# Fewer weights split ahead, their loads on another queue, and a new order of the attention and what follows

## The chip, the cores and the metric

The kernel runs on one core of one Trainium2 chip. The metric is the time of one execution on the device, in microseconds (us): before the change a median of 1505.86 us over three runs (1504.99 to 1508.77). Engines are named as in the profile: PE (TensorE, matmuls), PEld (its weight loads), DVE (VectorE), ACT (ScalarE), POOL (GpSimd) and SP (SyncE). SP and POOL start the transfers (DMAs); each takes its own in order and stands still when one has to wait.

## The reference

A model of two layers over 512 latent and 256 context tokens of width 1024 (one batch, fp32). Both layers normalise, scale and shift by a vector made from a condition, mix, project back and add to the residual:

```
for layer in range(2):
    sh, sc, ga = split(silu(c) @ w_mod[layer] + b_mod[layer])     # for latents, and for the context with c_ctx
    h = rms_norm(x, g_pre[layer]) * (1 + sc) + sh
    layer 0: xv, g_hy, q, k, v, g_att = split(h @ e_w_in)
             y = concat(hyena(xv) * silu(g_hy), attention(q, k, v) * silu(g_att)) @ e_w_out
    layer 1: q, k, v, o, z, gates = split(h @ o_w_in)
             y = (rms_norm(mlstm_forward + mlstm_backward) * silu(z)) @ o_w_out    # latents only
    x = x + ga * rms_norm(y, g_post[layer])
```

The attention has 8 query heads and 2 key and value heads of 128; `hyena` is a short convolution and a long one of the sequence's length; the mLSTM of layer 1 has 8 heads with keys of 128 and values of 256, computed in chunks, with `sigmoid(o)` on its output.

## The kernel before

Every fp32 product is made of three faster ones: both operands are split into a high part (fp32r) and the rest, and `mm3` (L1021) adds high by high, high by low and low by high. Activations are split as they come, weights once each: `split` (L1011) is a CAST on ACT and a subtraction on DVE. The usual way of a weight tile of 1024 x 256 is `load_w` (L1036): two loads of 512 KB by SP into one of three `wr` buffers, two casts of 128x1024 into `wh`, two subtractions into `wl`.

The work stands in regions: start, hyena (hy), attention (att), the output of layer 0 (out0), two parts of layer 1 (l1a, l1b) and its output (out1). Each region is first recorded and then issued by `play` (L999) in the order of a table, `ORDERS` (L157), a permutation of the recorded work over all engines at once; a second table, `SLOTS` (L736), says which buffer of a pool each tile takes. All rows of the profile thus have the line L1006, and an engine works in the order that the table gives it. A wait in front of one instruction holds all that stand behind it on that engine or queue.

In the attention, three more things run beside it: weights of the next region, the vectors of the condition (`w_mod`, 1 MB tiles loaded by SP in pairs named wh and wl, and used by PE as they are, in products into `pm`), and `split_ahead` (L1898). This takes weights of layer 1 (o_w_in, named `ow`) and splits them early, since layer 1 has less room on ACT and DVE. One block is two of the eight k-tiles of a head's tile: `G.dma_start` (POOL) loads 256 KB into one of three places in `yacc0`, which the attention does not need; at the next call ACT casts it and DVE subtracts, in place, and POOL writes both halves to `w_scratch` in memory, from which the place is free again. `ahead` (L1894) lists the blocks: (head h, tile t, k), from head 1 on, without the first four: 52 blocks. The loop of 24 attention steps calls it three times a step (L2094). In the rows a load is `yacc<-in_o_w_in`, the cast and the subtraction are `yacc<-yacc`, the write is `w_scratch<-yacc`.

Layer 1 reads these back by `load_split` (L2266), two transfers of 1 MB by SP, in `Head.load` (L2429, the tile with queries and keys) and `Head.load_v` (L2432, the values).

The attention's own chain is: products into `pj`, CAST to `PTh` on ACT, subtraction to `PTl` on DVE, products of both by PE. `qjunk` is a sum of squares that ACT makes for the norm of the queries, `qTh`/`qTl` are the split queries, `hdh`/`hdl` the probabilities, and `dec` is a result that SP writes to `y_scratch`. In the output stages `hf` is the scaled and shifted transposed input, `xn` the normalised one.

Of the kernel before, what the change touches and what calls it, by code (L numbers as in the profile page):

```python
# [14 lines left out]
P = 128  # L15
# [136 lines left out]
class Ctx:  # L152
# [669 lines left out]
        2,  # L822
    ],
    "mrow@5": [
        0, 1, 0, 1, 0, 1, 0, 1,
    ],
    "xt@9": [
        1, 0, 1, 0, 1, 0, 1,
# [81 lines left out]
def _body(tc, ins, outs):  # L910
# [1160 lines left out]
    for n in range(24):  # L2071
# [22 lines left out]
        for _ in range(3):  # L2094
            split_ahead()
# [734 lines left out]
```

## Time and profile before

| what | value |
|---|---|
| median of three runs | 1505.86 us |
| the profiled execution | 1511.4 us, span 1509.6 us |
| PE busy | 1459.5 us, 97% of the span |
| DVE, ACT, POOL busy | 1079.8, 788.6, 179.9 us |
| mean granted clock of the core | 0.992 |
| attention, 410 to 720 us of the span | PE 294.0, DVE 227.8, ACT 166.2, POOL 101.8 us busy |
| yacc casts and w_scratch writes | 52 and 104 |

Busy time is from the instructions of each engine. The span is the profiled execution from its first to its last instruction; the rest of its time lies around it. The granted clock is a share of the full 2.4 GHz, so 0.5 is 1.2 GHz. A matmul's end is modelled, so its duration overlaps the next one's start.

### The profile page before, as it was taken

To read this page: it belongs to the slowest core of one execution; us is meant where nothing else is said; L and a number is where in the kernel's file an instruction comes from. 1 tells how busy PE (TensorE), PEld (TensorE's weight loads), DVE (VectorE), ACT (ScalarE), POOL (GpSimd) and SP (SyncE) were. 2 spreads that over 40 slices of the span, in tenths; PEclk is the share of its full clock that TensorE was granted. 3 is DMA by queue.
4 is the path that set the end of the run, shared out by engine and by line. 5 is a ranking of instruction groups with operands and counts; after the bars stand their busy time and mean duration, and the time that the engine had idled before them with its cause. 6 is when DMAs were issued, how large, how long until landed. Compare 5 with 4: busy or idle time off the path is not lost.

```text
span 1509.6 us, 26392 instructions
## 1 busy us (share of the span) xinstructions
PE 1459.5 (97%) x10266; PEld 1335.3 (88%) x10266; DVE 1079.8 (72%) x1986; ACT 788.6 (52%) x1608; POOL 179.9 (12%) x297
## 2 busy tenths in 40 slices
PE   7999999999998998999999989999999999999997
PEld 5889999889997897888998779999999999988985
DVE  6688787887866777779424889776666878789445
ACT  6633344334445554556332557555446777778432
POOL 1101001101114343421000100000000101000000
PEclk9999999999999999999999999999999999999999
DMA  9788677779656677663463234887765657674561
GB/s 378 227 196 204 187 200 163 197 207 210 141 167 213 221 250 233 238 234 119 149 226 107 102 127 127 270 282 246 237 227 194 247 209 256 241 254 145 202 229 59
DMA packets 86990, 306.51 MB, mean 203 GB/s; under 512 B 10907, under 2 KB 19611, under 8 KB 80624
## 3 DMA queue, kind: packets, MB, share of 16 engines
q1 hardware_dynamic: 65816, 233.24, 44.5%
q0 software_dynamic: 20176, 70.40, 19.0%
q8 instruction: 81, 1.33, 0.3%
q10 hardware_dynamic: 872, 1.18, 0.2%
q14 instruction: 45, 0.37, 0.1%
HBM read 247.60 MB, written 103.32 MB: 232 GB/s over the span
## 4 chain that ended last, share of the span: by engine, by line
PE 73%; DVE 9%; DMA 7%; issue 4%; ACT 4%; POOL 2%; SPq 0%; POOLq 0%; DVEq 0%; ACTq 0%
PE pj L1006 54%; PE pm L1006 17%; DMA yacc<-in_o_w_in 3%; DMA w_scratch<-yacc 2%; DVE hh L1006 1%; PE s L1006 1%; DVE wl L1006 1%; POOL w_scratch L1006 1%; DMA oz_scratch<-so 1%; ACT wh L1006 1%; DVE yacc L1006 1%; DVE num L1006 1%; DVE cvo L1006 0%; ACT hf L1006 0%; DMA decay<-nc_scratch 0%
## 5 line engine op out<-in xcount | busy, mean ns | idle before, releaser
L1006 PE MATMUL pj<-hTh,wh 128*128 128x512 f32 (+1 forms) x832 | 287.1, 347 | 1.7 <-DVE qTl L1006 1.4
L1006 PE MATMUL pj<-wh,hTh 128*128 128x256 f32 (+2 forms) x1008 | 286.5, 291 | 1.8 <-ACT wh L1006 1.0
L1006 PE MATMUL pj<-wl,hTh 128*128 128x256 f32 (+2 forms) x1008 | 285.3, 290 | 2.0 <-DVE wl L1006 2.0
L1006 PE MATMUL pj<-hTl,wh 128*128 128x512 f32 (+1 forms) x832 | 285.8, 345 | 0.4 <-DVE hTl L1006 0.4
L1006 PE MATMUL pj<-hTh,wl 128*128 128x512 f32 (+1 forms) x832 | 285.7, 345 | 0.0
L1006 PE MATMUL pj<-wh,hTl 128*128 128x256 f32 (+2 forms) x1008 | 285.1, 290 | 0.0
L1006 DVE TENSOR_TENSOR wl<-wr,wh 128x1024 fp32r<-128x1024 f32 (+1 forms) x126 | 152.3, 1213 | 70.3 <-ACT wh L1006 70.2
L1006 PEld LDWEIGHTS pj<-wh,hTh 128*128 128x128 f32 x1008 | 189.3, 190 | 6.4 <-issue 1.6
L1006 PEld LDWEIGHTS pj<-wl,hTh 128*128 128x128 f32 x1008 | 189.8, 190 | 5.4 <-DVE wl L1006 2.6
L1006 PEld LDWEIGHTS pj<-wh,hTl 128*128 128x128 f32 x1008 | 189.4, 190 | 3.5 <-issue 1.7
L1006 ACT CAST wh<-wr 128x1024 fp32r<-128x1024 f32 (+1 forms) x126 | 130.0, 1042 | 91.5 <-PE pj L1006 53.1
L1006 PEld LDWEIGHTS pj<-hTh,wh 128*128 128x128 f32 x832 | 156.9, 189 | 19.8 <-issue 2.0
L1006 PEld LDWEIGHTS pj<-hTl,wh 128*128 128x128 f32 x832 | 157.3, 189 | 17.8 <-DVE hTl L1006 0.7
L1006 PEld LDWEIGHTS pj<-hTh,wl 128*128 128x128 f32 x832 | 156.9, 189 | 17.9
L1006 POOL DMA_DIRECT2D o_sums<-in_o_w_in x44 | 35.8, 819 | 322.6 <-DMA o_sums<-in_o_w_in 161.4
L1006 DVE TENSOR_TENSOR wl<-ch,wh 128x1024 fp32r<-128x1024 f32 x44 | 53.6, 1219 | 28.7 <-ACT wh L1006 28.7
L1006 POOL DMA_DIRECT2D w_scratch<-yacc x104 | 56.8, 549 | 88.3 <-DVE yacc L1006 43.3
L1006 POOL TENSOR_SCALAR_AFFINE_SELECT decay<-decay 128x512 f32<-128x512 f32 x16 | 13.2, 829 | 410.9 <-DMA decay<-nc_scratch 384.1
L1006 ACT CAST wh<-ch 128x1024 fp32r<-128x1024 f32 x44 | 46.0, 1046 | 29.5 <-PE pj L1006 9.8
L1006 ACT CAST PTh<-pj 128x384 fp32r<-128x384 f32 (+1 forms) x80 | 34.9, 459 | 37.8 <-PE pj L1006 37.4
L1006 DVE TENSOR_TENSOR PTl<-pj,PTh 128x384 fp32r<-128x384 f32 (+1 forms) x80 | 40.6, 524 | 14.2 <-ACT PTh L1006 13.8
L1006 DVE TENSOR_TENSOR yacc<-yacc 128x512 fp32r<-128x512 f32 x52 | 35.5, 686 | 18.0 <-ACT yacc L1006 18.0
(381 smaller groups left out, 3609.9 us busy)
## 6 DMA issues: line engine op xcount, KB each, us to landing
wr<-in_e_w_in SPq DMA_DIRECT2D x52, 512.0 KB, 5.7
w_scratch<-yacc POOLq DMA_DIRECT2D x104, 256.0 KB, 4.0
o_sums<-in_o_w_in POOLq DMA_DIRECT2D x44, 512.0 KB, 8.3
ch<-o_sums SPq DMA_DIRECT2D x33, 512.0 KB, 4.1
wr<-in_o_w_in SPq DMA_DIRECT2D x30, 512.0 KB, 5.2
yacc<-in_o_w_in POOLq DMA_DIRECT2D x52, 256.0 KB, 4.1
wh<-w_scratch SPq DMA_DIRECT2D x13, 1024.0 KB, 7.3
wl<-w_scratch SPq DMA_DIRECT2D x13, 1024.0 KB, 7.7
```

What stands on the lines that cost most here:

```text
L1006: x = fn(*a, **k)
```

## The change

- `ahead` holds heads 2 to 6 alone: 40 blocks where there were 52. The second tile of head 1 and both of head 7 are now loaded and split as other weights (`load_w`, with two more loads of 512 KB, casts and subtractions for each tile). `w_scratch` shrinks to five heads.
- The loads of the blocks are issued by SP; the writes stay with POOL. The program has 134 transfers on POOL where it had 210, and 480 on SP where it had 440.
- An attention step calls `split_ahead` twice instead of three times (before the order of the table).
- The tables of order of att, out0, l1a, l1b and out1, and many buffer numbers, are new. PE has the same matmuls.

```diff
     "att": [
-        75, 76, 77, 78, 79, 45, 46, 47, 48, 49, 50, 51, 52, 53, 54, 55, 56, 57, 58, 59, 60, 61, 62, 63, 64, 65, 66, 67, 68, 80, 81, 82, 83, 15, 16,
+        15, 16, 17, 18, 19, 20, 21, 22, 23, 24, 25, 26, 27, 28, 29, 30, 31, 32, 33, 34, 35, 36, 37, 38, 2, 0, 3, 45, 46, 47, 48, 49, 50, 51, 52, 53,
...
-    wsd = nc.dram_tensor("w_scratch", [8, 2, 2, P, KT, 256], F32).ap()
-    ahead = [(h, t, k) for h in range(1, 8) for t in range(2) for k in range(0, KT, 2)][4:]
+    wsd = nc.dram_tensor("w_scratch", [5, 2, 2, P, KT, 256], F32).ap()
+    ahead = [(h, t, k) for h in range(2, 7) for t in range(2) for k in range(0, KT, 2)]
...
-                G.dma_start(wsd[h, t, i][:, k:k + 2], f(x))
+                G.dma_start(wsd[h - 2, t, i][:, k:k + 2], f(x))
...
-            G.dma_start(f(lo), ow[4 * h + t][:, k:k + 2])
+            SP.dma_start(f(lo), ow[4 * h + t][:, k:k + 2])
...
-        for _ in range(3):
+        for _ in range(2):
...
-            SP.dma_start(f(x), wsd[h, t, i])
+            SP.dma_start(f(x), wsd[h - 2, t, i])
...
-            self.w = w_next if self.h == 1 else load_split(self.h, 0) if self.h else load_w(ow[0])
+            self.w = w_next if self.h == 1 else load_split(self.h, 0) if 1 < self.h < 7 else load_w(ow[4 * self.h])
...
-            self.wv = load_split(self.h, 1)
+            self.wv = load_split(self.h, 1) if 1 < self.h < 7 else load_w(ow[4 * self.h + 1])
```

Three places show how the instructions move. The first is SP's queue in the attention, around the first pair of `w_mod` tiles (wh_829 and wl_830; dec is written out ahead of them, wr are weights of later regions). Before:

```order
L1006 DMA wr_4606<-in_e_w_in 128x1024
L1006 DMA wr_4597<-in_e_w_in 128x1024
L1006 DMA y_scratch<-dec_4367 128x768
L1006 DMA wh_829_4553<-in_w_mod 128x2048
L1006 DMA wl_830_4554<-in_w_mod 128x2048
L1006 DMA wr_4652<-in_e_w_in 128x1024
```

And now, from this pair to the second one (wl_957 and wh_956):

```order
L1006 DMA y_scratch<-dec_4367 128x768
L1006 DMA wl_830_4554<-in_w_mod 128x2048
L1006 DMA wr_4606<-in_e_w_in 128x1024
L1006 DMA wh_829_4553<-in_w_mod 128x2048
L1006 DMA yacc_600_4321<-in_o_w_in 128x512 x2
L1006 DMA wr_4645<-in_e_w_in 128x1024
...
L1006 DMA yacc_600_4321<-in_o_w_in 128x512
L1006 DMA wr_4733<-in_e_w_in 128x1024
L1006 DMA wl_957_4681<-in_w_mod 128x2048
L1006 DMA yacc_600_4321<-in_o_w_in 128x512
L1006 DMA wh_956_4680<-in_w_mod 128x2048
L1006 DMA yacc_600_4321<-in_o_w_in 128x512 x4
```

The loads of the blocks stand among SP's transfers, two of them right behind the first pair, one between the two tiles of the second.

The second place is ACT in the attention, around the four casts into one PTh tile (PTh_4570; hdh and hdl are probabilities of one row of tokens). Before:

```order
L1006 CAST PTh_4570<-pj_4572 128x3x128
L1006 CAST PTh_4570<-pj_4573 128x3x128
L1006 CAST PTh_4570<-pj_4582 128x3x128
L1006 CAST yacc_600_4321<-yacc_600_4321 128x512
L1006 CAST PTh_4570<-pj_4581 128x3x128
L1006 CAST wh_871_4595<-wr_4597 128x1024
```

And now:

```order
L1006 CAST PTh_4570<-pj_4572 128x3x128
L1006 ACTIVATE hdh_4365,sm_4576<-s_850_4574,mx_4575,rq_4504 128x256
L1006 CAST yacc_600_4321<-yacc_600_4321 128x512
L1006 CAST PTh_4570<-pj_4573 128x3x128
L1006 ACTIVATE hdl_4366,sm_4585<-s_859_4583,mx_4584,rq_4504 128x256
L1006 CAST PTh_4570<-pj_4581 128x3x128
L1006 CAST PTh_4570<-pj_4582 128x3x128
```

A cast of a block still stands between the casts of one PTh tile, with three of these behind it where there was one.

The third place is DVE late in the heads of layer 1, at the end of a chunk (num is its numerator, dn its denominator, C and Cl the state of the mLSTM and its low part, vl the low part of values). Before:

```order
L1006 SCALAR_TENSOR_TENSOR dn_12958<-num_2231_12928 128x4
L1006 TENSOR_TENSOR dn_12958<-dn_12958,cq_1360_9530 128x4
L1006 RECIPROCAL dn_12958<-dn_12958 128x4
L1006 SCALAR_TENSOR_TENSOR C_12978<-C_12973,apb_9531,pj_12974 128x258
L1006 TENSOR_TENSOR Cl_12976<-C_12973,Ch_12975 128x258
L1006 TENSOR_TENSOR Cl_12981<-C_12978,Ch_12980 128x258
L1006 SCALAR_TENSOR_TENSOR C_12984<-C_12978,apb_9531,pj_12979 128x258
L1006 SCALAR_TENSOR_TENSOR C_12990<-C_12984,apb_9531,pj_12985 128x258
L1006 SCALAR_TENSOR_TENSOR num_2273_12970<-pm_12983,cq_1360_9530,num_2273_12970 128x258
```

And now:

```order
L1006 SCALAR_TENSOR_TENSOR dn_12900<-num_2233_12870 128x4
L1006 TENSOR_TENSOR dn_12900<-dn_12900,cq_1360_9470 128x4
L1006 RECIPROCAL dn_12900<-dn_12900 128x4
L1006 TENSOR_TENSOR wl_2310_12947<-wr_12949,wh_2309_12946 128x1024
L1006 TENSOR_TENSOR vl_12837<-pj_12907,vh_12836 128x256
L1006 SCALAR_TENSOR_TENSOR C_12915<-C_12911,apb_9471,pj_12914 128x258
L1006 SCALAR_TENSOR_TENSOR C_12920<-C_12915,apb_9471,pj_12916 128x258
L1006 TENSOR_TENSOR wl_2314_12951<-wr_12952,wh_2313_12950 128x1024
L1006 TENSOR_TENSOR Cl_12918<-C_12915,Ch_12917 128x258
```

Two of the four subtractions of head 7's raw weights (wl from wr) now stand in front of the state's low part; one stands 15 rows ahead of these, one 32 rows behind.

## Rows read from the trace of the kernel before

**Rows 1.** The page, part 1: busy us, share of the span, instructions.

```profile
PE 1459.5 (97%) x10266; PEld 1335.3 (88%) x10266; DVE 1079.8 (72%) x1986; ACT 788.6 (52%) x1608; POOL 179.9 (12%) x297
```

**Rows 2.** Busy us by stretch (instructions), then granted clock, DMA share, GB/s.

```profile
410.00:720.00 310.00, 294.01 (x2170) 270.90 (x2169) 227.75 (x512) 166.19 (x414) 101.80 (x168) 0.98 0.63 208
450.00:500.00 50.00, 45.09 (x292) 40.80 (x291) 32.02 (x69) 29.29 (x74) 19.79 (x34) 0.93 0.62 203
550.00:600.00 50.00, 45.44 (x347) 41.77 (x345) 36.07 (x88) 26.62 (x72) 16.48 (x31) 0.97 0.71 237
...
1320.00:1360.00 40.00, 38.94 (x264) 34.74 (x263) 34.04 (x75) 30.02 (x78) 3.16 (x7) 1.00 0.72 251
1360.00:1400.00 40.00, 38.45 (x298) 36.10 (x297) 38.60 (x90) 34.65 (x93) 1.94 (x2) 1.00 0.39 126
```

**Rows 3.** What PE waited for in the attention: us, times, longest.

```profile
PE pj L1006 <- DVE PTl L1006: 6.7, 3, 3.4
PE pj L1006 <- ACT qjunk L1006: 4.0, 9, 1.2
PE pj L1006 <- DVE qTl L1006: 1.4, 1, 1.4
```

**Rows 4.** PE around both long gaps: start, us, operation, idle time before.

```profile
487.39 0.58 PE L1006 MATMUL pj<-PTh,hw 128*128 128x256 f32 x1 [3.10 <-DVE PTl L1006]
487.77 0.42 PE L1006 MATMUL pj<-PTl,hw 128*128 128x256 f32 x1
...
577.44 0.39 PE L1006 MATMUL pj<-PTh,hw 128*128 128x256 f32 x1 [3.43 <-DVE PTl L1006]
577.66 0.28 PE L1006 MATMUL pj<-wh,hTl 128*128 128x256 f32 x1
577.78 0.28 PE L1006 MATMUL pj<-PTl,hw 128*128 128x256 f32 x1
```

**Rows 5.** ACT before both gaps, columns as before.

```profile
484.92 1.14 ACT L1006 CAST yacc<-yacc 128x512 fp32r<-128x512 f32 x2 [4.81 <-DMA yacc<-in_o_w_in]
...
574.98 0.62 ACT L1006 CAST yacc<-yacc 128x512 fp32r<-128x512 f32 x1 [4.50 <-DMA yacc<-in_o_w_in]
```

**Rows 6.** What ACT waited for in the attention, columns as for PE.

```profile
ACT yacc L1006 <- DMA yacc<-in_o_w_in: 24.1, 14, 4.8
```

**Rows 7.** POOL: one wait of the timeline, then the sum over the attention.

```profile
571.00 1.15 POOL L1006 DMA_DIRECT2D yacc<-in_o_w_in  x2 [10.42 <-DMA w_scratch<-yacc]
...
POOL yacc L1006 <- DMA w_scratch<-yacc: 66.9, 27, 10.4
```

**Rows 8.** DMAs in the attention: queue, number, KB, median us to landing.

```profile
yacc<-in_o_w_in POOLq DMA_DIRECT2D x52, 256.0 KB, 4.1
...
wh<-in_w_mod SPq DMA_DIRECT2D x3, 1024.0 KB, 7.7
wl<-in_w_mod SPq DMA_DIRECT2D x3, 1024.0 KB, 12.9
```

**Rows 9.** Block casts, subtractions, landing: ns or us min/median/max; splits of 128x1024: busy us, mean ns.

```profile
L1006 ACT CAST yacc<-yacc x52: 606/620/651, 432.7 to 676.1; 128x512 fp32r<-128x512 f32 x52
L1006 DVE TENSOR_TENSOR yacc<-yacc x52: 670/684/695, 433.7 to 682.2; 128x512 fp32r<-128x512 f32 x52
...
DMA to landing us min/median/max: 2.6/4.1/12.2
...
L1006 DVE TENSOR_TENSOR wl<-wr,wh 128x1024 fp32r<-128x1024 f32 (+1 forms) x126 | 152.3, 1213 | 70.3 <-ACT wh L1006 70.2
...
L1006 ACT CAST wh<-wr 128x1024 fp32r<-128x1024 f32 (+1 forms) x126 | 130.0, 1042 | 91.5 <-PE pj L1006 53.1
```

**Rows 10.** DVE behind the last matmul.

```profile
1499.56 0.68 DVE L1006 TENSOR_TENSOR yacc<-yacc,gg 128x512 f32<-128x512 f32 x1
1500.16 1.41 DVE L1006 SCALAR_TENSOR_TENSOR xt<-yacc,ers,xt 128x512 f32<-128x512 f32 x2
```

**Rows 11.** What PE waited for at the end of layer 0's output.

```profile
PE pm L1006 <- ACT hf L1006: 3.8, 4, 1.7
```

More of the change, by code (lines that the diff above doesn't have):

```diff
@@ L754 @@
     "pj@2": [
-        0, 1, 0, 1, 2, 3, 0, 2, 1, 3, 2, 0, 1, 3, 2, 0, 1, 3, 3, 0, 1, 2, 0, 3, 1, 1, 3, 1, 0, 2, 3, 1, 0, 2, 0, 1, 3, 2, 0, 1, 2, 3, 1, 3, 2, 0, 1,
-        3, 2, 0, 3, 1, 2, 0, 3, 1, 0, 2, 3, 1, 0, 2, 2, 1, 0, 3, 2, 1, 0, 0, 3, 2,
+        0, 2, 0, 2, 3, 1, 0, 3, 2, 1, 3, 0, 2, 1, 3, 0, 2, 1, 1, 0, 2, 3, 0, 1, 2, 2, 1, 2, 0, 3, 1, 2, 0, 3, 0, 2, 1, 3, 0, 2, 3, 1, 2, 1, 3, 0, 2,
+        1, 3, 0, 1, 2, 3, 0, 1, 2, 0, 3, 1, 2, 0, 3, 3, 2, 0, 1, 3, 2, 0, 0, 1, 3,
     ],
@@ L784 @@
     "rt@6": [
-        0, 1, 1, 1, 0, 1, 1, 0, 1, 0, 1, 0, 0, 0, 1, 0, 1, 1, 0, 1, 0, 1,
+        0, 1, 1, 1, 1, 0, 1, 0, 1, 0, 1, 0, 0, 1, 0, 0, 1, 0, 1, 0, 1, 0,
     ],
@@ L812 @@
     "s2@8": [
-        0, 1, 1, 0, 1, 1, 0, 1, 1, 0, 1, 1, 0, 1, 0, 1, 0, 0, 1, 0, 1, 0, 1, 0, 0, 1, 0, 1, 0, 1, 1, 1, 0, 0, 1, 0, 0, 1, 1, 0, 1, 0, 1, 0, 1, 0, 1,
+        0, 1, 0, 0, 1, 1, 0, 1, 1, 0, 1, 0, 1, 0, 1, 0, 1, 1, 1, 0, 1, 1, 0, 1, 0, 1, 0, 0, 1, 1, 0, 1, 1, 0, 1, 1, 0, 1, 1, 0, 1, 1, 0, 1, 0, 1, 1,
         0,
@@ L816 @@
     "mx@6": [
-        0, 3, 1, 2, 0, 3, 1, 2, 0, 3, 1, 0, 2, 3, 1, 0, 2, 3, 1, 0, 2, 3, 1, 0, 2, 3, 1, 0, 3, 2, 1, 0, 3, 2, 1, 0, 2, 3, 1, 0, 3, 2, 1, 0, 3, 2, 1,
-        0,
-    ],
-    "sm@6": [
-        0, 3, 1, 2, 3, 0, 1, 2, 3, 0, 1, 2, 3, 0, 1, 2, 3, 0, 1, 2, 3, 0, 1, 2, 3, 0, 1, 2, 3, 0, 1, 2, 3, 0, 2, 1, 0, 3, 2, 1, 0, 3, 1, 2, 0, 3, 1,
-        2,
-    ],
+        0, 3, 1, 0, 2, 1, 3, 0, 2, 0, 1, 3, 2, 0, 1, 3, 2, 0, 3, 1, 0, 1, 2, 3, 0, 2, 1, 0, 3, 2, 1, 0, 3, 2, 1, 3, 0, 2, 1, 3, 0, 2, 1, 3, 0, 2, 1,
+        3,
+    ],
+    "sm@6": [
+        0, 1, 3, 2, 0, 1, 3, 2, 0, 1, 3, 2, 0, 1, 2, 3, 0, 1, 3, 2, 0, 2, 1, 3, 0, 1, 2, 3, 0, 1, 2, 3, 0, 1, 2, 3, 0, 1, 2, 0, 3, 1, 2, 0, 3, 1, 2,
+        0,
+    ],
     "mrow@5": [
-        0, 1, 0, 1, 0, 1, 0, 1,
+        0, 1, 0, 1, 0, 1, 1, 0,
     ],
     "xt@9": [
-        1, 0, 1, 0, 1, 0, 1,
+        0, 1, 0, 1, 0, 1, 0,
     ],
     "pj@10": [
[5 rows of a table removed]
[5 rows of a table added]
     ],
     "pm@11": [
[5 rows of a table removed]
[5 rows of a table added]
     ],
     "yraw@9": [
-        0, 0, 0, 0, 1, 1, 0, 0,
+        0, 1, 0, 0, 1, 1, 0, 0,
     ],
@@ L859 @@
     "xn@9": [
-        0, 1, 2, 0, 1, 2, 0, 2, 0, 1, 2, 1,
+        0, 1, 0, 2, 1, 0, 1, 2, 0, 1, 2, 1,
     ],
@@ L868 @@
     "cvo@12": [
-        0, 1, 2, 0, 1, 2, 0, 1, 2, 0, 1, 2, 0, 1, 2, 0, 1, 2,
+        0, 1, 2, 0, 1, 2, 0, 1, 2, 0, 1, 2, 0, 1, 0, 1, 2, 0,
     ],
     "ch@13": [
-        0, 1, 0, 0, 1, 1, 0, 1, 0, 1, 0, 1, 0, 1, 0, 1, 0, 1, 0, 1, 0, 1, 0, 1, 0, 1, 0, 1, 0, 1, 0, 1, 0, 1, 0, 1, 0, 1, 0, 1, 0, 1, 0, 1,
+        0, 1, 0, 1, 0, 1, 0, 1, 0, 1, 0, 1, 0, 1, 0, 1, 0, 1, 0, 1, 0, 1, 0, 1, 0, 1, 0, 1, 0, 1, 0, 0, 1, 0, 0, 1, 0, 1, 0, 1, 0, 1, 0, 1,
     ],
     "decay@14": [
-        1, 0, 1, 0, 1, 0, 1, 1, 0, 1, 0, 1, 0, 1, 0, 1,
+        0, 1, 0, 0, 1, 0, 0, 1, 0, 0, 0, 1, 0, 1, 1, 0,
     ],
     "C@14": [
-        1, 0, 1, 0, 1, 0, 1, 0, 1, 0, 1, 0, 1, 0, 1, 0, 1, 0, 1, 0, 0, 1, 0, 1, 0, 0, 1, 0, 1, 0, 1, 0, 1, 0, 1, 0, 1, 0, 1, 0, 1, 0, 1, 0, 1, 0, 1,
-        0, 1, 0, 1, 0, 1, 0, 1, 0, 1, 0, 1, 0, 0, 1, 0, 1, 0, 1, 0, 1, 0, 1, 0, 1, 0, 1, 0, 1, 0, 1, 0, 1,
+        1, 0, 1, 0, 1, 1, 0, 1, 0, 1, 0, 1, 0, 1, 0, 1, 0, 1, 0, 1, 0, 1, 0, 1, 0, 1, 0, 1, 0, 1, 0, 1, 0, 1, 0, 1, 0, 1, 0, 1, 1, 0, 1, 0, 1, 0, 1,
+        0, 1, 0, 1, 0, 1, 0, 1, 0, 1, 0, 1, 0, 1, 0, 1, 0, 1, 0, 1, 0, 1, 0, 1, 0, 1, 0, 1, 0, 1, 0, 1, 0,
     ],
     "Ch@14": [
-        1, 0, 1, 0, 1, 0, 0, 1, 0, 1, 0, 1, 0, 1, 1, 0, 0, 1, 1, 0, 0, 1, 0, 1, 0, 1, 0, 0, 1, 0, 1, 0, 0, 1, 1, 0, 1, 0, 1, 0, 1, 0, 1, 1, 0, 1, 1,
-        0, 0, 1, 1, 0, 1, 0, 1, 0, 0, 1, 0, 1, 0, 1, 1, 0,
+        1, 0, 0, 1, 1, 0, 1, 0, 0, 1, 0, 1, 0, 1, 0, 1, 1, 0, 1, 0, 0, 1, 0, 1, 0, 1, 1, 0, 1, 0, 1, 0, 0, 1, 0, 1, 0, 1, 0, 1, 0, 1, 0, 1, 1, 0, 1,
+        0, 0, 1, 0, 1, 0, 1, 0, 1, 0, 1, 1, 0, 0, 1, 0, 1,
     ],
     "Cl@14": [
-        0, 1, 0, 1, 1, 0, 0, 1, 0, 1, 0, 1, 0, 1, 1, 0, 0, 1, 1, 0, 0, 0, 1, 0, 1, 0, 1, 1, 0, 1, 0, 1, 0, 1, 0, 1, 0, 1, 0, 1, 0, 1, 0, 0, 1, 0, 0,
-        1, 0, 1, 1, 0, 1, 0, 1, 0, 0, 1, 0, 1, 0, 1, 0, 1,
+        0, 1, 1, 0, 0, 1, 0, 1, 1, 0, 1, 0, 1, 0, 1, 0, 1, 0, 0, 1, 1, 0, 1, 0, 1, 0, 1, 0, 1, 0, 0, 1, 1, 0, 1, 0, 1, 0, 1, 0, 1, 0, 1, 0, 1, 0, 1,
+        0, 0, 1, 0, 1, 0, 1, 0, 1, 0, 1, 1, 0, 0, 1, 0, 1,
     ],
@@ L892 @@
     "yraw2@15": [
-        0, 2, 2, 3, 3, 1, 0, 1,
+        0, 1, 0, 1, 2, 3, 0, 2,
     ],
@@ L898 @@
     "esst@15": [
-        1, 0, 1, 0,
+        0, 1, 0, 1,
     ],
     "ers@15": [
-        1, 0, 1, 0,
+        0, 1, 1, 0,
     ],
     "xt@15": [
-        1, 0, 3, 2,
+        2, 3, 1, 0,
     ],
```

868 rows, old and new, of tables (ORDERS, SLOTS) are left out of this document.

## The prediction

> **What bounds the kernel now.** I read the page first: TensorE (PE) is busy 97% of the span [rows 1], so the matmuls themselves set the time and only what PE waits for, or does at half clock, can be won. The table of stretches says where that lies [rows 2]. The attention (410 to 720 us) has 294.0 us of PE work in 310.0: 16.0 us idle, a third of the 50 us idle in the whole span (1509.6 less 1459.5). Two of its stretches have a mean granted clock of 0.93 and 0.97, so 3.5 + 1.5 = 5.0 us of their matmul speed were lost as well.
>
> The waits tell what PE waited for there [rows 3]: 6.7 us for PTl in three waits, longest 3.4; 4.0 us for qjunk in nine small ones; 1.4 us once for qTl. The two long gaps, 3.10 and 3.43 us, end at 487.39 and 577.44 [rows 4]. After the first, matmuls 128x256 take 0.42 us, after the second 0.28, and follow each other by 0.12 us at full speed: the granted clock went from 2.4 to 1.2 GHz behind a gap. Now one engine back: ScalarE (ACT) works in order, and before both gaps it stood 4.81 and 4.50 us at a CAST of yacc whose load had not landed [rows 5]; PTh stood queued behind it, PTl on VectorE (DVE) behind PTh. In the attention ACT lost 24.1 us so, in 14 waits, none over 4.8 [rows 6]. One step further: of the second, the load was issued at 571.00 only because GpSimd (POOL) stood 10.42 us until the writes that freed its yacc slot had landed; 66.9 us went that way in 27 waits [rows 7].
>
> So the bound that the change touches is a chain: slot written out, load, cast, PTh, PTl, PE. By the second bound, DVE, the end of the layer 1 heads is close: 38.60 of 40 us busy from 1360 to 1400 [rows 2].
>
> **The change part by part.** I count everything against the profiled execution (1511.4 us, span 1509.6). It is 5.5 us above the median of 1505.86, so I apply the difference to the median and leave the two ends of the range to allow that unprofiled executions stall less.
>
> *Longer way from load to cast, in the attention.* Along the two orders I counted the matmuls between a block's load and its cast and took them at the trace's spacing (0.12 us for 128x256, others likewise). By this estimate a load of before has a median of about 5.2 us of matmul work ahead of its cast, one of after about 10.3; a slot's second write precedes the next load by about 2.7 us in both. Loads land in 4.1 us in the median [rows 8], loads and writes together too [rows 9], so the way takes 8.2: before grants 7.9, after 13.0. All 14 waits are shorter than the 5.1 us gained. If nothing else came in, the terms are 6.7 (PTl) + 1.4 (qTl) + 5.0 (clock) = 13.1 us, and 1 of the 4.0 us of qjunk, as ACT and DVE also lose 12 casts (620 ns) and 12 subtractions (684 ns) here [rows 9]: together −14.1. Not less than −6.5 (the two gaps alone), not more than −17.
>
> *The loads now on SP's queue.* There they stand behind SP's own transfers. The trace has the price: of two 1 MB w_mod loads issued one behind the other the first lands in 7.7 us, the second in 12.9 [rows 8]; each further MB costs 5.2. The order of SP shows two places. At the first pair a load follows 2.5 MB and its cast stands some 10 us of matmuls behind the start of these; I expect 7.7 + 5.2 × 1.75 = 16.8 us, so ACT waits about 6. At the second pair two loads stand beside the pair, late by some 4 and 2 us in the same way, and behind the first pair a slot is written out during the pair, about 3 more (writes beside the pair took up to 12.2 us [rows 9]). Sum 15 us of ACT waiting if the queue delivers strictly in turn, none if it shares as the POOL loads did. At 13.1 us of PE time per 24.1 us of waiting this is 0 to +8.2; I take the middle, +4.1, since in the trace the second of a pair was slower than the first but not by its whole 7.7.
>
> *The second w_mod pair itself.* PE needs both tiles. In before, the first use stands 13 us of matmuls behind the issue, about what the pair takes. In after wl goes first, a yacc load stands between, and wh, the last of a group of 3 MB (two loads, a half of weights, wl, wh), is used some 13 us behind the head of this group: strictly in turn it lands after 7.7 + 5.2 × 2 = 18.1, and PE would wait 5 us. Bounds 0 (the queue shares, or the group starts early) and 5; I take +2, nearer to none because SP can run ahead of the order's place.
>
> *Twelve blocks fewer split ahead.* 36 POOL transfers of 256 KB go, and in layer 1 six casts (1042 ns) and six subtractions (1213 ns) of whole halves come [rows 9]: 6.3 us on ACT, 7.3 on DVE. Two each (head 1) stand at the start of these heads, far from the full stretch, and I put them at nothing. Four each (head 7, near 1330 to 1360) meet DVE at 34.0 of 40, then 38.6 of 40 [rows 2]: 7.4 us free for 4.9. Zero if they fit the gaps, 5 if each stands in front of what PE waits for; I take +2.
>
> *End and out0.* After the last matmul and its add, DVE still does the gate product and two updates of the third tile, 0.68 + 1.41 us [rows 10]. In after these stand before it; the sum of squares still has to be waited for, so −0.9 (bounds 0 and −2). Layer 0's output stage keeps its chain over hf (3.8 us [rows 11]), other order: 0, ±2.
>
> Sum: −14.1 + 4.1 + 2 + 2 − 0.9 = −6.9, profiled 1504.5; median 1505.86 − 6.9 = 1499.
>
> **The rivals.**
> (a) *All waits go.* SP has issued the loads long before, as it only issues; the pairs share. Then −14.1 + 1 − 0.9 = −14: 1492. For it: the median load has twice the way, and SP, which only issues, may be far ahead of its place. Against: the 12.9.
> (b) *SP's queue gives the loads in turn,* and the attention gets back most of its loss: −14.1 + 8.2 + 5 + 2 − 0.9 = +0.2: 1506, no change. For it: 12.9 behind 7.7 [rows 8], the same at each pair. Against: only 5 of 40 loads stand right behind a w_mod tile. The Trainium skill, "DMA: Bandwidth & Descriptors" (section "Queues, rings and completion order"), says that each DMA engine takes a queue's descriptors in ring order and goes round between queues packet by packet: on POOL's queue a small load shared with SP's large ones, on SP's it stands behind them. By that rule the result is this rival's 1506, without it (a)'s; the trace agrees for SP's own pair, and shows no small load behind one.
> (c) *Slower: a held slot holds SP.* SP issues in order. The yacc load between wl and wh waits until its slot is written out; POOL stood 10.42 us for this beside a pair [rows 7], with nothing behind it that PE needed at once. If SP stands so, wh goes out 10.4 us after wl, lands 7.7 later, 18.1, where PE wants it after about 9 behind wl: a gap of 9 us and, as after the gap before, 3.5 us of clock. With (b)'s other terms: −14.1 + 8.2 + 12.5 + 2 − 0.9 = +7.7: 1514. It decides from about 4 us of waiting at that row on, and ends slower from about 8. Against it: that slot's writes stand 9 us of matmuls ahead.
> (d) *The order does nothing:* the two stalls fall elsewhere, as landing times vary. Same as (b) in time.
>
> **How the numbers follow.** Forecast 1499, own range 1493 to 1503: 0.53. (a) 0.10, (b) with (d) 0.22, (c) 0.15. A measurement of this kernel tells 0.3% (4.5 us) from no change: faster is below 1501.3, slower above 1510.4. Of the forecast four fifths are below 1501.3; with (a) and a little of (b) that is 0.55. The rest of the forecast and most of (b): 0.28. Slower is (c) and a tail: 0.17. The range reaches from 1489 (a with the lower bounds) to 1510, and leaves most of (c) and a little below out.
>
> **What would show it.** Right: in the attention, PE idle falls from 16 to about 9 us; ACT's waits for yacc from 24.1 to about 8, and what is left stands behind w_mod pairs; no gap over 3 us away from them; granted clock 0.98 or more in all its stretches but one; SP now waits for w_scratch to land. Wrong: waits for yacc spread over the attention as before (then landing grew with the way); PE waiting for wh or wl in its pm products by over 5 us (c); idle at 1320 to 1400 grown by over 4 us (the splits of head 7 meet a full DVE); or the gain sits in a stage that I put at nothing, above all out0.

## The result and the profile after

The changed kernel takes 1499.19 us (median of five runs, 1498.83 to 1500.46) where the kernel before takes 1508.77 beside it (1504.99 to 1511.76): a ratio of 0.994, 95% interval 0.992 to 0.996. It is faster by 9.6 us. The forecast was 1499. In these five runs the kernel before stood 2.9 us above the three from which the forecast started, so the time was met and the saving (6.9 forecast) was put 2.7 us too small.

The page, part 1, of the kernel after (busy us, share of the span, instructions), beside [rows 1]:

```profile
PE 1457.6 (97%) x10266; PEld 1333.6 (89%) x10266; DVE 1081.3 (72%) x1980; ACT 788.8 (53%) x1602; POOL 139.3 (9%) x221
```

The span is 1498.7 us. TensorE's work has not changed, so what it loses shows as idle time (the length of a stretch less PE's busy time), by stretch as in [rows 2]:

```profile
410.00:720.00 310.00, 303.21 (x2283) 281.57 (x2281) 229.14 (x517) 165.80 (x415) 60.02 (x92) 0.99 0.55 182
450.00:500.00 50.00, 49.60 (x357) 45.81 (x356) 35.72 (x80) 26.96 (x72) 8.50 (x13) 1.00 0.50 158
550.00:600.00 50.00, 49.80 (x391) 46.10 (x390) 39.50 (x94) 29.30 (x77) 11.73 (x18) 1.00 0.68 228
650.00:700.00 50.00, 47.99 (x344) 42.75 (x343) 40.14 (x89) 32.99 (x70) 12.82 (x19) 0.97 0.81 264
```

In the attention PE is idle for 6.8 us where it was 16.0, and the two stretches that had a granted clock of 0.93 and 0.97 have 1.00. Now 650 to 700 has 0.97 (1.00 before). What PE still waits for there, as in [rows 3]:

```profile
PE pj L1006 <- DVE dec L1006: 1.7, 1, 1.7
PE pj L1006 <- DVE PTh L1006: 1.4, 1, 1.4
PE pj L1006 <- DVE PTl L1006: 0.9, 2, 0.7
PE pj L1006 <- ACT qjunk L1006: 0.7, 2, 0.5
```

PTl fell from 6.7 us to 0.9; the two longest waits left are for dec and PTh, other work of DVE. One engine back, ACT and SP (beside [rows 6, 7]), and then ACT at its three remaining waits (start, us, operation, idle before):

```profile
ACT yacc L1006 <- DMA yacc<-in_o_w_in: 4.0, 3, 1.6
SPq L1006 <- DMA w_scratch<-yacc: 163.9, 27, 14.4
```

```profile
560.12 0.62 ACT L1006 CAST yacc<-yacc 128x512 fp32r<-128x512 f32 x1 [1.64 <-DMA yacc<-in_o_w_in]
624.28 0.62 ACT L1006 CAST yacc<-yacc 128x512 fp32r<-128x512 f32 x1 [0.96 <-DMA yacc<-in_o_w_in]
659.55 0.62 ACT L1006 CAST yacc<-yacc 128x512 fp32r<-128x512 f32 x1 [1.36 <-DMA yacc<-in_o_w_in]
```

The three stand behind the `w_mod` tiles, as forecast. SP's queue around the second pair shows the load of the second wait, between the two tiles; the last row is the load of the third:

```profile
614.20 0.42 SPq L1006 DMA_DIRECT2D wl<-in_w_mod  x1
614.72 0.40 SPq L1006 DMA_DIRECT2D yacc<-in_o_w_in  x1
615.17 0.88 SPq L1006 DMA_DIRECT2D wh<-in_w_mod  x1
...
650.39 0.37 SPq L1006 DMA_DIRECT2D yacc<-in_o_w_in  x1
```

The load between the two tiles was issued at once, 8.6 us before ACT was ready for it, and did not hold wh. It landed after 9.48 us, over twice the median of these loads, at 624.20, and ACT took it at 624.28 after 0.96 us of waiting. PE waited for no `w_mod` tile. Issues of the attention, with KB and median us to landing, beside [rows 8]:

```profile
w_scratch<-yacc POOLq DMA_DIRECT2D x80, 256.0 KB, 3.3
yacc<-in_o_w_in SPq DMA_DIRECT2D x40, 256.0 KB, 4.3
wl<-in_w_mod SPq DMA_DIRECT2D x3, 1024.0 KB, 6.0
wh<-in_w_mod SPq DMA_DIRECT2D x3, 1024.0 KB, 8.8
```

The trace has the landing of every write here, but on SP's queue only of 12 of the 40 block loads, of one wl and of two wh; those medians are of these.

Outside the attention little was won. The windows and waits give PE's idle time by region, before to after: start 9.7 to 10.1, out0 8.4 to 9.2, the heads of layer 1 from 4.3 to 6.3, the end 10.7 to 7.9.

### The profile page after: what moved, and what is told of

Same layout as the page of the kernel before. It is cut to its first block, busy times and chain, and to the rows that moved or that the text cites. A ratio compares the mean times of both kernels' runs of the same rounds, so it can differ in the third digit from the quotient of the medians.

```text
span 1498.7 us, 26290 instructions
## 1 busy us (share of the span) xinstructions
PE 1457.6 (97%) x10266; PEld 1333.6 (89%) x10266; DVE 1081.3 (72%) x1980; ACT 788.8 (53%) x1602; POOL 139.3 (9%) x221
## 5 line engine op out<-in xcount | busy, mean ns | idle before, releaser
L1006 DVE TENSOR_TENSOR wl<-wr,wh 128x1024 fp32r<-128x1024 f32 x132 | 159.3, 1213 | 64.9 <-ACT wh L1006 64.6
L1006 ACT CAST wh<-wr 128x1024 fp32r<-128x1024 f32 x132 | 136.6, 1044 | 71.9 <-PE pj L1006 52.1
L1006 POOL DMA_DIRECT2D w_scratch<-yacc x80 | 44.0, 552 | 176.6 <-DVE yacc L1006 83.4
L1006 DVE TENSOR_TENSOR PTl<-pj,PTh 128x384 fp32r<-128x384 f32 (+1 forms) x80 | 40.6, 524 | 14.2 <-ACT PTh L1006 13.9
L1006 PE MATMUL pm<-Rh,dfa 128*128 128x256 f32 (+1 forms) x192 | 45.0, 305 | 0.0
```

What stands on the lines that cost most here:

```text
L1006: x = fn(*a, **k)
```

## The experiments

Medians are of four to twelve runs. Each experiment stands beside runs of the kernel before on the same chip; the ratio is to these.

**The attention alone.** `e1` takes the kernel after for the attention and the kernel before for every other region. Since those regions expect split weights that are no longer made, head 1's second tile and head 7 read another head's.

```diff
 ORDERS, SLOTS: "att" of after; start, hy, out0, l1a, l1b, out1 of before
...
+            SP.dma_start(f(x), wsd[min(max(h - 2, 0), 4), t, i])   # in load_split
...
```

> The attention of after (its order, 40 blocks, loads on SP) with the orders of before in out0, l1a, l1b and out1. The values of head 1 and both tiles of head 7 are read from other heads' places in w_scratch, so layer 1 does before's transfers with other numbers. Theory (the attention alone holds the gain; the rest of after costs 0.8 in out0 and 3.7 in l1b and gives back 2.8 at the end, by the two traces): about 12 us below before, 1495 to 1499, attention idle about 7 us. Rival (the rest holds a good part of the gain): 1502 to 1506, slower than after.

Measured: 1496.88 us, ratio 0.992 (0.991 to 0.993), 12.4 us under the kernel before. The attention holds the whole gain. By the medians the rest of the change costs 2 to 3 us, but the runs of `e1` (1495.82 to 1501.35) overlap those of the kernel after.

**The heads of layer 1 and the end, each added to it.** `e2` is `e1` with the l1b region of after (so its weights are right again), `e3` is `e1` with the out1 region of after.

```diff
 e2: "l1b" of after;   e3: "out1" of after
...
+            self.wv = load_split(self.h, 1) if 1 < self.h < 7 else load_w(ow[4 * self.h + 1])   # e2
```

> The same, with after's l1b too (head 7 and the values of head 1 split from raw weights there). Theory (in l1b four casts and four subtractions more stand in a full DVE): 3 to 4 us above the kernel with the attention alone, with the waits for hh, num and wl and a half-clock stretch near the end of the heads. Rival (l1b's idle time comes from landings and varies): within 1 us of it.

> The attention of after and its order of out1, all else from before (values of head 1 and head 7 from other places, as in the first). Theory (the last tile's chain is shorter): 2 to 3 us below the kernel with the attention alone, DVE's work behind the last matmul down from 4.5 to about 3 us. Rival (only the gate product of 0.68 us is saved, the rest is the difference of two profiles): under 1 us.

Measured: `e2` 1500.69, ratio 0.994 (0.992 to 0.995), so l1b costs 3.8 us by the medians. The runs of the two kernels overlap (`e2` has 1498.02 to 1501.75), but the traces say the same: PE is idle for 4.5 us in these heads in `e1` and for 7.3 in `e2`. `e3` 1497.70, ratio 0.9915 (0.990 to 0.993): its rival was right, the new end gains nothing that can be measured. In its trace it is 7.8 us from DVE's last add to the end, where `e1` has 8.8.

**No loads at all.** `e4` is the kernel before with 49 of its 52 block loads left out, `e7` the kernel after with 37 of its 40; casts, subtractions and writes stay and work on what lies in the buffer.

```diff
-            G.dma_start(f(lo), ow[4 * h + t][:, k:k + 2])
+            if len(ahead) >= 49:          # e7: SP, and 37
+                G.dma_start(f(lo), ow[4 * h + t][:, k:k + 2])
...
```

> Before, without 49 of the 52 block loads; casts, subtractions and writes stay and work on what lies in the places. Theory (PE's idle time in the attention comes from casts that wait for a load): ACT's 24.1 us of such waits gone, attention idle 3 to 6 us, no half-clock stretch there, 1492 to 1498. Rival (before's order itself makes the stalls, or the slots that the writes hold): attention idle over 11 us, above 1502.

> After, without 37 of the 40 block loads; casts, subtractions and writes stay. Theory (in after the loads are hidden but for 4.0 us of ACT waiting in three places behind w_mod tiles, none of which stopped PE): 1497 to 1500, within 1.5 us of after, PE idle in the attention still 6 to 7 us. Rival (SP, which stands 163.9 us for w_scratch in the attention, holds up transfers that PE needs): 1493 to 1496, idle under 4 us.

Measured: `e4` 1495.16, ratio 0.990 (0.989 to 0.9915); `e7` 1499.12, ratio 0.994 (0.993 to 0.995), the time of the kernel after itself. The stretch 410 to 720 of `e4`, then of `e7`:

```profile
410.00:720.00 310.00, 304.45 (x2309) 283.12 (x2308) 238.72 (x537) 173.33 (x430) 74.14 (x119) 1.00 0.51 173
```

```profile
410.00:720.00 310.00, 303.68 (x2291) 282.42 (x2290) 229.87 (x518) 165.86 (x415) 59.98 (x92) 0.99 0.43 151
```

Without the loads the old attention loses 5.6 us instead of 16.0: waiting for loads was its loss, with the old order and the casts, subtractions and writes of all 52 blocks. In the kernel after nothing is left to win from them.

**The queue apart from the order.** `e5` is the kernel after with its loads on POOL again; `e6` the kernel before with its loads on SP.

```diff
 e5, from after:                                         e6, from before:
-            SP.dma_start(f(lo), ow[...][:, k:k + 2])    -            G.dma_start(f(lo), ow[...][:, k:k + 2])
+            G.dma_start(f(lo), ow[...][:, k:k + 2])     +            SP.dma_start(f(lo), ow[...][:, k:k + 2])
```

> After, with the block loads issued by POOL as in before; orders unchanged. Theory (what counts is the longer way from load to cast in the order, not the queue): 1497 to 1503, ACT's waits for yacc loads at most 8 us, PE idle in the attention at most 9 us. Rival (the loads had to leave POOL, where they wait for a slot with the next writes behind them): over 1504, ACT's waits over 15 us again.

> Before, with the block loads issued by SP as in after; orders unchanged. Theory: the way of 5.2 us stays shorter than write and load, ACT's waits stay between 15 and 35 us, time 1504 to 1512, more if SP's own transfers are held up. Rival (the queue is the cause): ACT's waits under 8 us, below 1502.

Measured: `e5` 1517.0, ratio 1.007 (1.005 to 1.008): slower than the kernel before by 9.4 us. `e6` 1500.2, ratio 0.996 (0.994 to 0.997): one line gives 7.4 us. My theory, that the longer way does it and the queue does not matter, fell twice. In `e6` ACT still waits 15.2 us for block loads, but never over 2.9, and PE's wait for PTl falls from 6.7 to 1.9. In `e5` PE waits 10.7 us for PTl, 10.5 of it in two gaps. The rows of `e5` around its longer gap are ACT, then PE, then POOL:

```profile
667.38 0.62 ACT L1006 CAST yacc<-yacc 128x512 fp32r<-128x512 f32 x1 [7.25 <-DMA yacc<-in_o_w_in]
```

```profile
669.25 0.90 PE L1006 MATMUL pj<-c_ident,dfb 128*128 128x128 f32 x3 [6.30 <-DVE PTl L1006]
```

```profile
652.00 1.07 POOL L1006 DMA_DIRECT2D w_scratch<-yacc  x2 [3.05 <-DVE yacc L1006]
657.36 0.54 POOL L1006 DMA_DIRECT2D w_scratch<-yacc  x1 [4.29 <-DVE yacc L1006]
657.89 1.07 POOL L1006 DMA_DIRECT2D yacc<-in_o_w_in  x2
```

Read from below: POOL stood for DVE's subtraction at a write; the load stood behind that write, waited for nothing else, went out at 657.89 within 2 us of two `w_mod` tiles, and took 9.47 us. ACT was ready for it at 660.13, 2.2 us after the issue. In the kernel after, where no write stands ahead of it on SP, the load of this block goes out 9.9 us ahead of its cast (643.64 and 653.59) and is not waited for. The other gap of `e5` (4.18 us at 631.71) is of the same kind: 5.8 us from issue to ACT's being ready where the kernel after has 8.6, and 9.88 us to landing. The median way from issue to cast is 9.7 us in `e5`, 9.9 in the kernel after, 5.4 in the kernel before. The median was as long as forecast, and PE lost as much as before: the two loads that came late set most of it.

In the kernel before POOL's waits in the attention had it, below the row of [rows 7]:

```profile
POOL w_scratch L1006 <- DVE yacc L1006: 43.3, 16, 21.4
POOL w_scratch L1006 <- ACT yacc L1006: 32.4, 17, 4.5
```

At these writes POOL stood for 75.7 us in all, with loads queued behind, which I had not weighed.

**The queues changed about.** `e9` tells whether SP's queue is quicker in itself, or whether the loads only had to leave POOL's writes behind. It is the kernel before with the loads left on POOL and the writes on SP.

```diff
-                G.dma_start(wsd[h, t, i][:, k:k + 2], f(x))
+                SP.dma_start(wsd[h, t, i][:, k:k + 2], f(x))
```

> The kernel before with POOL and SP changed about in the attention: the block loads stay on POOL's queue, and the writes to w_scratch go to SP's; all orders of the engines are unchanged. Theory: a load was late in the kernel before because it stood in POOL's queue behind other writes, which wait for casts and subtractions. With the writes gone from that queue only the slot holds a load, as when the loads were on SP (1500.2, ACT waiting 15.2 us for yacc, PE 301.6 us busy in 410 to 720). So: ACT's waits for yacc fall from 24.1 to 10 to 18 us, none over 3.5, PE 299 to 303 busy there, and 1498 to 1503. Rival: SP's queue itself lands a load sooner or starts it sooner than POOL's; then the waits stay at 20 to 28 us with two gaps of PE over 3 us, and the time at 1505 to 1511. A second rival: the writes, which wait for DVE, now hold SP's other loads (weights, context tiles, w_mod) behind them; then PE waits for wr, wh or wl and the time is above 1511.

Measured: 1499.15, ratio 0.994 (0.992 to 0.996). The theory held, with less waiting than it said. SP's queue does not land a load sooner: the median is 4.3 us on POOL here and 3.8 on SP in `e6` (18 of 52 landings in the trace), against 4.1 on POOL in the kernel before. ACT's wait and the attention of `e6`, then of `e9`:

```profile
ACT yacc L1006 <- DMA yacc<-in_o_w_in: 15.2, 10, 2.9
410.00:720.00 310.00, 301.59 (x2258) 278.97 (x2258) 233.22 (x526) 169.80 (x425) 72.58 (x116) 0.99 0.66 213
```

```profile
ACT yacc L1006 <- DMA yacc<-in_o_w_in: 8.4, 9, 2.2
410.00:720.00 310.00, 302.19 (x2272) 279.05 (x2271) 235.16 (x529) 171.90 (x425) 47.08 (x64) 1.00 0.68 215
```

Whichever of the two moves, loads and writes in different queues give about 7 to 9 us with the old order. SP stood at writes for the casts and subtractions in `e9` (44 waits, none over 6.8 us), and PE did not feel it.

What belongs to the attention can be read from the same work in five traces, from PE's 2552nd matmul to its 5031st, with the columns of [rows 2]: the kernel before, `e5`, `e6`, `e9` and the kernel after.

```profile
405.11:751.19 346.08, 330.09 (x2481) 306.32 (x2484) 246.00 (x553) 178.44 (x442) 101.80 (x168) 0.99 0.62 201
406.93:751.65 344.72, 328.50 (x2482) 305.16 (x2484) 238.77 (x541) 171.32 (x429) 81.55 (x132) 0.98 0.54 174
405.21:740.44 335.23, 326.82 (x2481) 303.74 (x2484) 245.65 (x553) 177.42 (x442) 72.58 (x116) 0.99 0.64 208
406.97:740.55 333.58, 325.77 (x2482) 302.16 (x2485) 245.92 (x553) 178.50 (x442) 47.08 (x64) 1.00 0.66 209
405.51:737.44 331.93, 325.14 (x2482) 302.96 (x2484) 239.15 (x541) 171.51 (x429) 60.02 (x92) 0.99 0.56 181
```

PE is idle for 16.0, 16.2, 8.4, 7.8 and 6.8 us of these. With the old order, loads and writes on different queues shorten the stretch by 10.9 and 12.5 us. The new order with both on POOL shortens it by 1.4. On top of the different queues the new order, with its twelve blocks fewer, is worth 1.7 to 3.3. Each row is one execution, and the runs of `e6` alone spread over 6 us, so the small differences are not shown; no run tells the order from the fewer blocks. Nearly all of the gain is there with one line changed. And of the +9.4 of `e5`, which has the other new orders too, the heads of layer 1 have 3.8 by `e2`.

**Room for the twelve blocks elsewhere.** If l1b costs 3.8 us, a kernel with the new attention and the old rest could stand at 1497, if the twelve blocks were split in layer 0's output stage. `e8` does this there with the load and the writes on POOL and one block for each 38 matmuls, in the three `xn` buffers; `e10` issues each load 19 matmuls earlier, ahead of the writes of the block before. Both compute the whole reference. (The conditions are put side by side here; `e8` writes them a little differently.)

```diff
+        if held and seen[0] % 38 == 0:                # cast, subtraction, both writes of a block
+            h, t, k, hi, lo = held.pop(0)
...
+        if more and seen[0] % 38 == 0:                # e8: its load, behind these writes
+        if more and (seen[0] % 38 == 19 or seen[0] == 1):   # e10: half a step earlier
...
+            keep(G.dma_start(f(lo), ow[4 * h + t][:, k:k + 2]))
```

> The attention of after and the other orders of before; the twelve blocks that after no longer splits ahead (values of head 1, head 7) are split in layer 0's output stage instead, one per 38 matmuls, in the three places of xn, which lie idle until that stage's end, loads and writes on POOL. Theory (DVE is 47.6 of 120 us busy there, ACT 38.9, POOL idle, so the splits are hidden, and layer 1's heads stay as in before): 1495.5 to 1498.5, 1 to 4 us below after, no new waits of PE from 720 to 838. Rival (casts and subtractions stand in front of weights or yoh that PE waits for, or their 9 MB of transfers hold up y_scratch loads): 1500 to 1505.

> A version that computes the whole reference: the attention alone in its new order with its loads on SP, every other region in the old order and on split weights, and the twelve blocks that the attention no longer does (second tile of head 1, both of head 7) loaded, cast, subtracted and written in layer 0's output stage, one for each 38 matmuls, in three buffers. Before, with the load one step of about 8 us of PE ahead of its cast and behind the writes on POOL, this took 1518.3 us, with ACT standing 3.7 to 6.9 us at four casts. Now each load is issued half a step earlier, ahead of the writes of the block before: some 12 us of PE ahead of its cast. Theory (a load is late when it stands behind writes that wait for casts and subtractions): the stands of ACT at these casts fall below 2 us each, the stage loses 3 us at most, and the time is 1497 to 1502. Rival: the stage has no room for 36 transfers of 256 KB beside its own w_mod pairs and weights, and their landing grows: 1504 to 1518, with PE waiting for wl or wh of w_mod.

Measured: `e8` 1518.25, ratio 1.007 (1.006 to 1.008). `e10` 1511.97, ratio 1.002 (1.001 to 1.0035). What ACT waited for in the stage (us, times, longest), in `e8` and then in `e10`:

```profile
ACT xs L292 <- DMA xs<-in_o_w_in: 24.0, 5, 6.9
```

```profile
ACT xs L292 <- DMA w_scratch<-xs: 19.5, 6, 5.9
```

`e8` missed its forecast by 20 us. It made the stall of the kernel before once more: a load behind writes in POOL's order, a cast that waits, PE behind it. In `e10` no wait for a load is left, as the theory said, but the time it gave for that did not come: with three buffers for two halves a block, the cast now waits for the writes of an earlier block to land. The wait had only changed its name. Its rival is borne out in part: the time lies in its range, PE waited 2.6 us for one wl and 1.0 for one wh, for which it does not wait in `e1` without the blocks, and the weight loads of the stage (`wr`) landed in 5.8 us in the median where `e1` has 4.3 (6 of 11 landings in each trace). Which of the two cost more is open.

**What costs in the heads of layer 1.** `e11` lets POOL do head 7's four subtractions; `e12` cuts them to 8 of 256 columns, head 7 using the high part in the low part's place.

```diff
 e11:                                                 e12:
-        return V.tensor_tensor(lo, src, f(hi), ...)  -                split(hi[:, sl, :256], lo[:, sl, :256], raw)
+        return (eng or V).tensor_tensor(...)         +                S.copy(hi[:, sl, :256], raw)
+   load_w(ow[4 * self.h], eng=G)   # head 7 alone    +                V.tensor_tensor(lo[:, sl, :8], ...)
```

> The kernel after with the four subtractions of head 7's raw weights (128x1024, 1.22 us each on DVE at 1317.9 to 1344.9) done by POOL, at the same places of the order. The heads of layer 1 cost the kernel after 3.8 us (1496.9 with the attention alone, 1500.7 with these heads too). Theory: that cost is DVE's, which is busy 36 of 40 us there (34.0 in the kernel before) and runs late behind them until the gaps at 1371.9 to 1398.1; then 2 to 4 us come back: 1495 to 1497.5, better than both kernels, with PE idle there 4.3 to 5 us instead of 6.3. Rival: the gaps stand 27 to 53 us behind the last of the four and come from the new order alone: 1498.5 to 1500.5. Second rival: POOL takes far longer than 1.22 us for one, stands in its order behind waits for PE, or holds DVE up; wl comes late for head 7's products, PE waits for it by over 3 us, and the time is above 1502.

> The kernel after with head 7's four subtractions cut to an eighth of a tile's row each (8 of 256 columns of each of four k-tiles); the products of head 7 take the high part in the low part's place, so its keys, queries and values lack the correction. All else is as in the kernel after, loads and casts of these weights too. It takes POOL's own price out of the question: only DVE's 4 x 1.2 = 4.8 us go. Theory (the 3.8 us of layer 1's heads are DVE's work): 1495 to 1497, idle of PE in these heads 4.3 to 5 us and the half-clock stretch at 1398 gone. Rival (the new order's gaps, whatever DVE has to do): 1498.5 to 1500, with gaps of 0.5 to 1.0 us at 1371, 1387 and 1396 as now.

Measured: `e12` 1498.83, ratio 0.9935 (0.992 to 0.995): the rival was right, the cost is not DVE's 4.8 us. `e11` 1504.24, ratio 0.997 (0.996 to 0.998), slower than the kernel after by 5 us, for its second rival in part. The last two gaps of these heads, in the kernel after and then in `e12`:

```profile
1396.28 0.50 PE L1006 MATMUL pj<-wl,hTh 128*128 128x256 f32 x2 [0.85 <-DVE wl L1006]
1398.06 1.43 PE L1006 MATMUL pm<-c_ident,hh 128*128 128x128 f32 x6 [0.68 <-DVE hh L1006]
```

```profile
1398.72 0.50 PE L1006 MATMUL pj<-wl,hTh 128*128 128x256 f32 x2 [0.86 <-DVE wl L1006]
1400.50 0.88 PE L1006 MATMUL pm<-c_ident,hh 128*128 128x128 f32 x6 [0.68 <-DVE hh L1006]
```

They are the same to 0.01 us with and without the subtractions. So are the gaps of 0.99 and 0.53 us at 1371.93 and 1387.11. The wl there is of the last weights, not of head 7. The kernel before has 0.25 and 0.26 us at these two matmuls. The stretch at half clock behind 1398 (granted clock 0.94 from 1390 to 1420) is gone in `e12`, but `e2`, with all of DVE's subtractions, has 1.00 there too. So what costs is not DVE's work on head 7's weights. Whether it is the new order of l1b, the casts and the 512 KB loads that `e12` still has, or head 1's splits, no run separates.

## Why the prediction came out right

*The bound.* Right from the load on: load, cast, PTh, PTl, PE was the attention's loss. `e4` gets 14.2 us by leaving out loads alone. What stood ahead of the load was put down to the slot; in `e9` POOL still stands 48.9 us for slots (13 waits, up to 7.7), and PE loses little by it.

*The longer way, −14.1.* The size was near, and the signs named came true (idle 6.8 where 9 was said, ACT's waits 4.0 where 8 was said, no gap over 3 us). The cause was wrong. The step that failed is "All 14 waits are shorter than the 5.1 us gained": it adds the gain to a way whose start stays where the order puts it. On POOL the start did not stay there. The order without the queue gains nothing: `e5` loses 9.4 us, and its attention is as idle as before.

*The loads on SP, +4.1.* The wrong sign. I had this edit as the price of the change, and it is the larger part of the gain: −7.4 with the old order (`e6`). I had read [rows 7] as a wait for the slot, 66.9 us, and not asked what POOL's other 75.7 us held up. The price was also misread: 7.7 and 12.9 in [rows 8] are not one pair. The trace has two landings of these six tiles, wl, second of the pair at 557 us, in 12.9, and wh, first of the pair at 633 us, in 7.7; 5.2 us for each further MB, and "the same at each pair" in rival (b), are not measured. With both edits the attention gives −12.4 (`e1`), against −14.1 + 4.1 + 2 = −8.0 in the sum. The parts do not add up: +9.4 (`e5`) and −7.4 (`e6`) would be +2.0, and the kernel after, which has both, is at −9.6.

*The second pair, +2.* Nothing: SP had wl and wh out within 1 us of each other, and PE waited for neither.

*Twelve blocks fewer, +2.* It cost 3.8 (`e2`), inside the bounds of 0 and 5, but not by head 7's subtractions on a full DVE, the reason given (`e12`); the cause stays open.

*The end, −0.9, and out0, 0.* The chain behind the last matmul is shorter by 1.0 us in the traces (`e3` beside `e1`). DVE there, beside [rows 10]: the gate product and the two updates of the third tile, which stood behind the last add, now stand ahead of it (1487.07 and 1488.20), and only the last tile's own stand behind:

```profile
1490.87 0.69 DVE L1006 TENSOR_TENSOR yacc<-pj,yacc 128x512 f32<-128x512 f32 x1 [1.26 <-PE pj L1006]
1492.41 0.16 DVE L1006 TENSOR_REDUCE ess<-ss 128x1 f32<-128x2 f32 x1 [0.85 <-ACT junk L1006]
1492.60 0.15 DVE L1006 TENSOR_SCALAR esst<-ess 128x1 f32<-128x1 f32 x1
1492.67 0.68 DVE L1006 TENSOR_TENSOR yacc<-yacc,gg 128x512 f32<-128x512 f32 x1
1493.80 1.41 DVE L1006 SCALAR_TENSOR_TENSOR xt<-yacc,ers,xt 128x512 f32<-128x512 f32 x2 [0.45 <-POOL ers L1006]
```

Out0's idle time is 0.8 us more. Both are too small for the runs.

*The sum.* −12.4 + 3.8 − 1.0 + 0.8 = −8.8 by the experiments and rows, −9.6 between the medians, −6.9 forecast. The attention's gain was put 4.4 us too low and l1b 1.8 too cheap. That the time came out at 1499 is luck in part: what the separate queues gave was put down to the longer way, the queue itself was counted as a price, the errors of the attention and of l1b partly offset each other, and the kernel before was 2.9 us slower in the later runs.

*The rivals.* What came is nearest to (a) in the attention, with l1b's cost on top. (b): the Trainium skill, "DMA: Bandwidth & Descriptors" (section "Queues, rings and completion order"), has each DMA engine take a queue's descriptors in ring order and go round between queues packet by packet. By that a small load behind large ones on its queue would land late, and the 9.48 us behind wl on SP's queue agree; but on POOL's queue, beside `w_mod` tiles on SP's, two loads took 9.88 and 9.47 (`e5`), so no gain from sharing shows in these three. What differed was how early they were issued. (c): the load between wl and wh had nothing to wait for, and SP's 163.9 us of standing held up nothing that PE needed: without the loads (`e7`) the time is the same. (d): true of the order with its loads on POOL (`e5`), where two stalls of PE stand at 631 and 669 us instead of 487 and 577; with loads and writes apart the order adds at most a few us.

No version that computes the whole reference is clearly faster than the kernel after. `e9`, the kernel before with the writes on another queue, has the same time with one line changed.

## What to carry to other kernels

An engine's DMA queue works in order, so ask of each load what stands ahead of it on its queue and which engine that waits for; writes that wait for compute and loads that should run ahead belong on different queues. A longer distance in an engine's order is worth nothing where the start of the transfer is set by another queue's waits: read issue times, not only distances. And take an order and a queue apart before crediting either, over the same work: here the queue alone gave −7.4 us, the new orders alone +9.4, and both −9.6.

## What the runs showed of the hardware

In `e11` POOL took 2.4 to 3.0 us for a subtraction of 128x1024 where DVE takes 1.22, and DVE operations beside it were held up. POOL's rows, then DVE's:

```profile
1321.95 2.95 POOL L1006 TENSOR_TENSOR wl<-wr,wh 128x1024 fp32r<-128x1024 f32 x1 [0.32 <-ACT wh L1006]
...
1344.95 2.58 POOL L1006 TENSOR_TENSOR wl<-wr,wh 128x1024 fp32r<-128x1024 f32 x1 [1.53 <-ACT wh L1006]
```

```profile
1322.74 2.46 DVE L1006 TENSOR_TENSOR Cl<-C,Ch 128x258 fp32r<-128x258 f32 x1
...
1344.84 3.75 DVE L1006 SCALAR_TENSOR_TENSOR hh<-hh,hrs,zs 128x256 f32<-128x256 f32 x3
```

Cl takes 0.42 us elsewhere and one hh 0.48; here Cl ended 0.3 us after POOL did. The three hh were late by 2.3 us, PE waited 1.73 us for hh at 1347.88, and the granted clock of 1350 to 1390 fell to 0.96. The Trainium skill, "SBUF — State Buffer" (section "SBUF: two separate sides"), says that a DVE operation with two inputs in SBUF and a GpSimd operation that reads SBUF lock a shared port: the one that starts first has it for its whole instruction, and the other waits. These rows agree. DVE lost by this (2.0 + 0.8 + 2.3 us at three places) as much as the four subtractions had cost it.
